# RMSNorm on one core: the fourth tile stored whole, the third loaded in two halves, five rows of the last group on GpSimd

## The chip, the core and the metric

The kernel runs on one NeuronCore of a Trainium2 chip. The metric is device time in microseconds (us); before the change the median of 8 runs is 161.97 us, from 161.75 to 163.17. A core has a matrix engine (TensorE, PE), a vector engine (VectorE, DVE), a scalar engine (ScalarE, ACT), GpSimd (POOL), a sync engine (SyncE, SP) that here only issues transfers, and 16 DMA engines that carry all transfers between the off-chip memory (HBM) and the on-chip memory (SBUF). PSUM is the small memory that TensorE writes to.

## The reference

```python
def reference(x, gamma):          # x: (16, 1024, 512) float32, gamma: (512,) float32
    eps = 1e-5
    rms = np.sqrt(np.mean(x ** 2, axis=-1, keepdims=True) + eps)
    return (x / rms * gamma).astype(np.float32)
```

There are 16,384 rows of 512 numbers. Each is divided by its root mean square and multiplied by gamma, element by element. 33.55 MB are read and as much is written.

## The kernel before

**Tiles.** The rows are cut into 4 tiles of 128 partitions x 32 rows x 512 numbers, 8.39 MB each. A partition's 32 rows lie one after another in HBM, 64 KB in one piece. There are three buffers, `slots`; tiles 0, 1 and 2 (called first, second and third below) have one each, and tile 3 (the fourth) reuses the buffer of tile 0 (`slot_of`, line 86).

**Groups.** Compute goes by groups of rows of one tile, listed in `groups` (lines 75 to 85) as tile, first row, number of rows, the pieces in which squares are taken, and `share`: how many of the last rows of the group GpSimd scales. The first tile has groups of 7, 9 and 16 rows, the others two of 16 each.

**One group.** ScalarE squares a piece of rows into a scratch tile, and VectorE sums each row of it (`square_sums`, lines 92 and 93). ScalarE takes the root, and VectorE the reciprocal (`inverse_rms`, lines 98 and 99). GpSimd then multiplies its share of the rows by the reciprocals, and in a second pass by gamma (lines 105 and 106). ScalarE multiplies the other rows by their reciprocal, one instruction for each row (line 114), and when all of these are done, VectorE multiplies them by gamma in one instruction (line 118), which reads gamma from PSUM. While a group is scaled, squares and sums of the next group are mixed in between by the main loop (lines 162 to 178); in the last group nothing is left to mix in.

**Gamma.** It is loaded in five pieces into one partition (lines 53 to 57), spread over 128 partitions by a matmul with a column of ones (line 66), and copied from PSUM to SBUF for GpSimd (line 161).

**Order.** The schedule is manual: every engine's instructions stand in the order of the program, and semaphore waits are added where data depend. All transfers are issued by SP, in program order, so an issue that waits holds all later ones. The first loads are issued at once; all further stores and loads are issued by `transfers` (lines 125 to 145), called after a group's work is written down. After the first group it issues three single-row stores of the first tile between the loads of the third tile, which comes as one half and two quarters. After the third group it issues the stores of the rest of the first tile, and then the loads of the fourth tile into the same buffer, which wait for these stores to have landed. The second and third tile are each stored whole; the fourth is stored in two halves, each after its own group.

Of the kernel before, what the change touches and what calls it, by code (L numbers as in the profile page):

```python
# [9 lines left out]
def kernel(  # L10
# [15 lines left out]
    N, D = xf.shape  # L26
# [17 lines left out]
    def load(t, slot, r0, r1):  # L44
        dma = nc.sync.dma_start(out=slots[slot][:, r0:r1], in_=xv[t][:, r0:r1])
        before_scale.append((slot, r0, r1, dma))

    def store(t, slot, r0, r1):
        dma = nc.sync.dma_start(out=ov[t][:, r0:r1], in_=slots[slot][:, r0:r1])  # L49
        before_scale.append((slot, r0, r1, dma))  # L50

    gamma_row = const.tile([1, D], fp32)
    pieces = (0, 128, 224, 320, 416, D)

    load(0, 0, 0, 8)
    for c0, c1 in zip(pieces, pieces[1:]):
# [24 lines left out]
        (2, 0, 16, (7, 5, 4), 7),  # L81
        (2, 16, 16, (7, 5, 4), 7),
        (3, 0, 16, (7, 5, 4), 7),
        (3, 16, 16, (7, 5, 4), 3),
    ]
    slot_of = [0, 1, 2, 0]

    def square_sums(ss, t, g, r, m, k):
        home, name, most = ((psum, "sq_psum", 7), (const, "sq_sbuf", 5))[k % 2]
        sq = home.tile([P, most, D], fp32, name=name)  # L90
        rows = slots[slot_of[t]][:, g + r : g + r + m, :]
        nc.scalar.activation(out=sq[:, :m], in_=rows, func=AF.Square)  # L92
        nc.vector.tensor_reduce(  # L93
            out=ss[:, r : r + m, 0], in_=sq[:, :m], axis=mybir.AxisListType.X, op=OP.add
        )

    def inverse_rms(ss, n):
        nc.scalar.activation(out=ss[:, :n, 0], in_=ss[:, :n, 0], func=AF.Sqrt, bias=eps_t, scale=1.0 / D)  # L98
        nc.vector.reciprocal(out=ss[:, :n, 0], in_=ss[:, :n, 0])  # L99
        return ss  # L100

    def scale_by_pool(rstd, t, g, n, share):
        part = slots[slot_of[t]][:, g + n - share : g + n, :]
        by_row = rstd[:, n - share : n].to_broadcast([P, share, D])
        nc.gpsimd.tensor_tensor(out=part, in0=part, in1=by_row, op=OP.mult)  # L105
        last = nc.gpsimd.tensor_tensor(  # L106
            out=part, in0=part, in1=gamma_b.to_broadcast([P, share, D]), op=OP.mult
        )
        before_scale.append((slot_of[t], g + n - share, g + n, last))

    def scale(rstd, t, g, r0, r1):
        x = slots[slot_of[t]]
        for r in range(r0, r1):
            nc.scalar.activation(out=x[:, g + r, :], in_=x[:, g + r, :], func=AF.Copy, scale=rstd[:, r])  # L114

    def times_gamma(t, g, r0, r1):
        part = slots[slot_of[t]][:, g + r0 : g + r1, :]
        scaled = nc.vector.tensor_tensor(  # L118
            out=part, in0=part, in1=gamma_psum.to_broadcast([P, r1 - r0, D]), op=OP.mult
        )  # L120
        for slot, b0, b1, earlier in before_scale:
            if slot == slot_of[t] and b0 < g + r1 and g + r0 < b1:
                tc.declare_no_dep(scaled.ins, earlier.ins, reason="ScalarE waited for it before it scaled these rows")

    def transfers(t, g):
        if (t, g) == (0, 0):
            store(0, 0, 0, 1)
            load(2, 2, 0, 16)
            store(0, 0, 1, 2)
            load(2, 2, 16, 24)  # L130
            store(0, 0, 2, 3)
            load(2, 2, 24, 32)
        elif (t, g) == (0, 16):
            store(0, 0, 3, 16)
            store(0, 0, 16, 32)
            load(3, 0, 0, 16)
            load(3, 0, 16, 32)
        elif (t, g) == (1, 16):
            store(1, 1, 0, 32)
        elif (t, g) == (2, 16):  # L140
            store(2, 2, 0, 32)
        elif (t, g) == (3, 0):
            store(3, 0, 0, 16)
        elif (t, g) == (3, 16):
            store(3, 0, 16, 32)

    def pieces_of(group):
        t, g, n, pieces, share = group
        ss = stats.tile([P, 16, 1], fp32, name="ss")
        r = 0  # L150
        todo = []
        for k, m in enumerate(pieces):
            todo.append((ss, t, g, r, m, k))
            r += m
        return ss, todo
# [6 lines left out]
    for k, group in enumerate(groups):  # L162
        t, g, n, pieces, share = group
        mine = n - share
        half = (mine + 1) // 2
        ahead = groups[k + 1 :][:1]
        ss, todo = pieces_of(ahead[0]) if ahead else (None, [])
        scale_by_pool(rstd, t, g, n, share)
        for piece in todo[:2]:
            square_sums(*piece)  # L170
        scale(rstd, t, g, 0, half)
        for piece in todo[2:]:
            square_sums(*piece)
        scale(rstd, t, g, half, mine)
        times_gamma(t, g, 0, mine)
        transfers(t, g)
        for nxt in ahead:
            rstd = inverse_rms(ss, nxt[2])
# [30 lines left out]
```

## Time and profile before

| | before |
|---|---|
| median of 8 runs | 161.97 us |
| the profiled execution | 162.09 us, with a span of 160.1 us |
| busy share DVE / ACT / POOL | 70% / 68% / 66% |
| HBM read, written | 33.56 MB, 33.55 MB |
| mean rate of DMA over the span | 419 GB/s |
| DMA packets' share of 16 engines' span | 98.2% |
| SP's issues for the fourth tile's stores | 123.3 us and 137.97 us |

The span runs from the first to the last instruction of the profiled execution; the device time is some 2 us longer. Times inside the span count from its start. Busy shares are means over the whole span. The DMA rows tell how much of 16 engines' time had packets in it. A packet is one contiguous piece moved by one DMA engine: here one partition's part of one transfer. Issuing a transfer takes SP about 0.4 us; "to landing" is the time from the issue until the completion arrived.

### The profile page before, as it was taken

What the parts mean: (1) busy time and instruction counts of PE and PEld (TensorE: products, weight loads), DVE (VectorE), ACT (ScalarE), POOL (GpSimd) and SP (SyncE); (2) the same over time, 40 slices, a digit from 0 to 9 for tenths busy, and PEclk for the clock granted to TensorE, in tenths of its full rate; (3) what the DMA queues carried; (4) which work ended last, traced back from release to release, by engine and by line L of the source; (5) the groups of instructions that cost most, each with busy time, mean ns of one, the idle gap of its engine ahead of it and who ended that gap; (6) DMA issues with size and microseconds to landing.
All of it is one profiled execution on the core that took longest, in us unless ns stands there. A gap on an engine that the chain in (4) does not pass through costs nothing.

```text
span 160.1 us, 280 instructions
## 1 busy us (share of the span) xinstructions
PE 2.0 (1%) x2; PEld 0.5 (0%) x2; DVE 112.5 (70%) x42; ACT 108.1 (68%) x111; POOL 106.4 (66%) x24
## 2 busy tenths in 40 slices
PE   0050000000000000000000000000000000000000
PEld 0010000000000000000000000000000000000000
DVE  0018597997989999999999999899996039400000
ACT  3072989859999998998999499999933960000000
POOL 1000956986998699999999999999999930000000
DMA  5999999999999999999999999996996997999994
GB/s 194 426 438 483 426 393 450 467 393 393 459 393 404 448 442 398 452 410 508 409 393 467 450 393 393 524 508 278 524 508 278 524 475 311 393 475 442 393 450 205
DMA packets 2747, 67.12 MB, mean 419 GB/s; under 512 B 313, under 2 KB 314, under 8 KB 698
## 3 DMA queue, kind: packets, MB, share of 16 engines
q1 hardware_dynamic: 2746, 67.11, 98.2%
q14 instruction: 1, 0.01, 0.0%
HBM read 33.56 MB, written 33.55 MB: 419 GB/s over the span
## 4 chain that ended last, share of the span: by engine, by line
DMA 38%; DVE 29%; ACT 16%; issue 2%; ACTq 0%; SPq 0%
DMA out_dram<-slot 21%; DMA slot<-in_x_dram 17%; DVE ss L93 17%; DVE slot L118 12%; ACT slot L114 8%; ACT sq_psum L92 6%; ACT sq_sbuf L92 1%; ACTq L204 0%; ACT ss L98 0%; ACT gamma_b L161 0%; DVE ss L99 0%; SPq L49 0%; ACTq L92 0%
## 5 line engine op out<-in xcount | busy, mean ns | idle before, releaser
L105 POOL TENSOR_TENSOR slot<-slot,ss 128x3584 f32<-128x3584 f32 (+2 forms) x9 | 46.9, 5214 | 21.9 <-DVE ss L99 21.9
L93 DVE TENSOR_REDUCE ss<-sq_psum 128x7 f32<-128x3584 f32 (+1 forms) x16 | 49.1, 3072 | 16.5 <-ACT sq_psum L92 16.4
L106 POOL TENSOR_TENSOR slot<-slot,gamma_b 128x3584 f32<-128x3584 f32 (+2 forms) x9 | 59.2, 6583 | 0.7
L114 ACT ACTIVATE slot<-slot,ss 128x512 f32<-128x512 f32 x75 | 47.4, 706 | 4.7 <-DVE ss L99 4.7
L118 DVE TENSOR_TENSOR slot<-slot,gamma_psum 128x4608 f32<-128x4608 f32 (+2 forms) x9 | 41.3, 4591 | 8.5 <-ACT slot L114 8.5
L92 ACT ACTIVATE sq_psum<-slot 128x3584 f32<-128x3584 f32 (+1 forms) x16 | 40.2, 2511 | 8.4 <-DMA slot<-in_x_dram 7.0
L93 DVE TENSOR_REDUCE ss<-sq_sbuf 128x5 f32<-128x2560 f32 x8 | 22.5, 2807 | 0.0
L92 ACT ACTIVATE sq_sbuf<-slot 128x2560 f32<-128x2560 f32 x8 | 18.6, 2321 | 0.0
L98 ACT ACTIVATE ss<-ss,eps_t 128x16 f32<-128x16 f32 (+2 forms) x9 | 2.7, 303 | 8.4 <-DVE ss L93 8.4
L99 DVE RECIPROCAL ss<-ss 128x16 f32<-128x16 f32 (+2 forms) x9 | 2.1, 236 | 0.4 <-ACT ss L98 0.4
L66 PE MATMUL gamma_psum<-gamma_row,ones_col 1*128 1x512 f32 x2 | 2.0, 1122 | 9.0 <-DMA gamma_row<-in_gamma_dram 9.0
L72 ACT ACT_TABLE_LOAD x1 | 1.3, 1283 | 1.2 <-PEq L193 1.2
L161 ACT COPY gamma_b<-gamma_psum 128x512 f32<-128x512 f32 x1 | 0.6, 567 | 0.0
L66 PEld LDWEIGHTS gamma_psum<-gamma_row,ones_col 1*128 1x128 f32 x2 | 0.5, 305 | 9.0 <-issue 9.0
L64 POOL MEMSET ones_col<- 1x128 f32 x1 | 0.2, 194 | 0.3 <-POOLq L193 0.3
L193 POOL MEMSET const-float32-0.0<- 128x1 f32 x1 | 0.1, 98 | 0.2 <-issue 0.2
L72 ACT ACTIVATE table<-eps_t 128x1 f32<-128x1 f32 x1 | 0.2, 202 | 0.0
L193 POOL MEMSET const-bfloat16-1.0<- 128x1 bf16 x1 | 0.1, 101 | 0.0
L193 POOL MEMSET const-uint8-127<- 128x1 uint8 x1 | 0.1, 101 | 0.0
L193 POOL MEMSET const-float32-1.0<- 128x1 f32 x1 | 0.1, 98 | 0.0
L70 POOL MEMSET eps_t<- 128x1 f32 x1 | 0.1, 89 | 0.0
## 6 DMA issues: line engine op xcount, KB each, us to landing
slot<-in_x_dram SPq DMA_DIRECT2D x6, 4096.0 KB, 21.9
out_dram<-slot SPq DMA_DIRECT2D x3, 4096.0 KB, 23.8
slot<-in_x_dram SPq DMA_DIRECT2D x4, 2048.0 KB, 10.2
out_dram<-slot SPq DMA_DIRECT2D x1, 3328.0 KB, 34.3
out_dram<-slot SPq DMA_DIRECT2D x3, 256.0 KB, 31.7
gamma_row<-in_gamma_dram SPq DMA_DIRECT2D x4, 0.4 KB
out_dram<-slot SPq DMA_DIRECT2D x2
gamma_row<-in_gamma_dram SPq DMA_DIRECT2D x1, 0.5 KB
```

The lines of the kernel that those rows point to most:

```text
L66: nc.tensor.matmul(gamma_psum[:, 0], ones_col, gamma_row, start=True, stop=True)
L72: nc.scalar.activation(out=table, in_=eps_t, func=AF.Sqrt)
L92: nc.scalar.activation(out=sq[:, :m], in_=rows, func=AF.Square)
L93: nc.vector.tensor_reduce(out=ss[:, r : r + m, 0], in_=sq[:, :m], axis=mybir.AxisListType.X, op=OP.add)
L98: nc.scalar.activation(out=ss[:, :n, 0], in_=ss[:, :n, 0], func=AF.Sqrt, bias=eps_t, scale=1.0 / D)
L99: nc.vector.reciprocal(out=ss[:, :n, 0], in_=ss[:, :n, 0])
L105: nc.gpsimd.tensor_tensor(out=part, in0=part, in1=by_row, op=OP.mult)
L106: last = nc.gpsimd.tensor_tensor(out=part, in0=part, in1=gamma_b.to_broadcast([P, share, D]), op=OP.mult)
L114: nc.scalar.activation(out=x[:, g + r, :], in_=x[:, g + r, :], func=AF.Copy, scale=rstd[:, r])
L118: scaled = nc.vector.tensor_tensor(out=part, in0=part, in1=gamma_psum.to_broadcast([P, r1 - r0, D]), op=OP.mult)
L161: nc.scalar.copy(out=gamma_b[:, 0], in_=gamma_psum[:, 0])
L193: nc = _bacc.Bacc("TRN2", target_bir_lowering=False, num_devices=1)
```

## The change

Four things are changed. Gamma is loaded in seven pieces instead of five, one of 128 numbers and six of 64. Of the three single-row stores after the first group two stay, the third row goes with the next store of that tile, and rows 16 to 31 of the third tile are loaded in one transfer instead of two. The store of the first half of the fourth tile is dropped, and the whole tile is stored after the last group. In the last group GpSimd takes five rows instead of three, and VectorE multiplies the other eleven by gamma in two instructions, of six rows and of five, the first placed after ScalarE's first six rows.

```diff
-    pieces = (0, 128, 224, 320, 416, D)
+    pieces = (0, 128, 192, 256, 320, 384, 448, D)
...
-        (3, 16, 16, (7, 5, 4), 3),
+        (3, 16, 16, (7, 5, 4), 5),
...
             store(0, 0, 0, 1)
             load(2, 2, 0, 16)
             store(0, 0, 1, 2)
-            load(2, 2, 16, 24)
-            store(0, 0, 2, 3)
-            load(2, 2, 24, 32)
+            load(2, 2, 16, 32)
         elif (t, g) == (0, 16):
-            store(0, 0, 3, 16)
+            store(0, 0, 2, 16)
             store(0, 0, 16, 32)
             load(3, 0, 0, 16)
             load(3, 0, 16, 32)
...
-        elif (t, g) == (3, 0):
-            store(3, 0, 0, 16)
         elif (t, g) == (3, 16):
-            store(3, 0, 16, 32)
+            store(3, 0, 0, 32)
...
         scale(rstd, t, g, 0, half)
+        if not ahead:
+            times_gamma(t, g, 0, half)
         for piece in todo[2:]:
             square_sums(*piece)
         scale(rstd, t, g, half, mine)
-        times_gamma(t, g, 0, mine)
+        times_gamma(t, g, 0 if ahead else half, mine)
         transfers(t, g)
```

## The prediction

> **What bounds the kernel now.** I read the page's slices of the span first. The rows are engines, each digit the busy tenths of a 4 us slice:
>
> ```profile
> DVE  0018597997989999999999999899996039400000
> ACT  3072989859999998998999499999933960000000
> POOL 1000956986998699999999999999999930000000
> DMA  5999999999999999999999999996996997999994
> GB/s 194 426 438 483 426 393 450 467 393 393 459 393 404 448 442 398 452 410 508 409 393 467 450 393 393 524 508 278 524 508 278 524 475 311 393 475 442 393 450 205
> ```
>
> The compute engines start late and stop five slices before the end. DMA is full from the second slice to the last but one; the few sixes sit beside slices over the mean and are not gaps, as the stretches below explain. Next the page's part on queues:
>
> ```profile
> DMA packets 2747, 67.12 MB, mean 419 GB/s; under 512 B 313, under 2 KB 314, under 8 KB 698
> q1 hardware_dynamic: 2746, 67.11, 98.2%
> ```
>
> 98.2% of 160.1 us is 157.2 us of packet time on each of 16 engines. The trace's single packet records begin at 1.74 us and end at 158.90, which is 157.16 us: no engine is ever without a packet in between.
>
> The chain of waits points elsewhere. Its last pieces (start, length, what) are
>
> ```profile
> 122.73 1.33 ACT slot L114 x2
> ...
> 124.67 6.13 ACT slot L114 x10
> 130.80 0.02 issue
> 130.82 7.09 DVE slot L118
> ```
>
> It is followed back from the last instruction and stops at 137.9; the 22 us behind it are not in it. What they are is shown by the table of stretches (the last two columns are DMA share and GB/s):
>
> ```profile
> 110.00:137.00 27.00, 0.00 (x0) 0.00 (x0) 18.87 (x6) 15.15 (x23) 19.35 (x4) 1.00 1.06 461
> 137.00:138.00 1.00, 0.00 (x0) 0.00 (x0) 0.91 (x1) 0.00 (x0) 0.00 (x0) 1.00 0.15 66
> 138.00:158.00 20.00, 0.00 (x0) 0.00 (x0) 0.00 (x0) 0.00 (x0) 0.00 (x0) 1.00 0.97 419
> 158.00:159.00 1.00, 0.00 (x0) 0.00 (x0) 0.00 (x0) 0.00 (x0) 0.00 (x0) 1.00 0.01 0
> ```
>
> A packet is booked whole to the stretch it starts in, so shares over 1 occur and a thin us is no gap. 20 us at 419 GB/s are 8.38 MB: all of the fourth tile (8.39 MB), the half issued at 123.3 as well as the half issued at 137.97. So the third tile's store kept the engines until about 138.9 (its 64 KB packets take 2.42 us each, and the last start just after 136 to 137), and the half issued at 123.3 had waited 15 us in the queue. The bound is bytes over the DMA engines, not the arithmetic.
>
> **What the Trainium skill says.** "DMA: Bandwidth & Descriptors", section "Where 436 GB/s comes from": 16 ports give 435 GB/s, and for transfers between HBM and SBUF a lower HBM limit of about 358 binds. The trace sides with the first: share 1.00 goes with 428 to 435 GB/s. The same page, "Why small descriptors are slow (HBM only)": a packet has a fixed overhead. The trace agrees: 24.4 GB/s per engine in 2 KB packets, 26.8 in 16 KB, 27.0 in 32 KB, 27.1 in 64 KB. The same page, "Why a DMA increments its semaphore by 16 and not by 1": a DMA runs on k engines set by its outer dimension, each ending with a semaphore write. The count of 313 small packets agrees: 19 large DMAs x 16, plus 5 + 4 for gamma's pieces on one engine.
>
> **The change part by part,** against the profiled span of 160.1 us (first packet at 1.74, last at 158.90, 1.2 us to the end). That execution took 162.09 us, 0.12 above the median of 161.97. Packet lengths are medians of the packet records: 84 ns for 2 KB, 611 for 16 KB, 987 for 26 KB, 1213 for 32 KB, 2418 for 64 KB, 9 for a semaphore write. Each engine carries 8 of a DMA's 128 packets.
>
> *Gamma in 7 pieces instead of 5.* SP issues five in 1.58 us (timeline), so two more cost 0.63 us, and every later issue of the first batch moves: the next load goes out at 3.4 instead of 2.79. It is hidden by the first load, whose packets last until 7.1 to 7.7; without that cover 0.63 us would be lost. On the one engine that carries gamma, a piece with its semaphore takes 25 ns in the records: +0.05 us, and that engine ends last, I infer from its order in the records. Matmul L66, which waits until 9.03, moves by the same; its product is read at 15.40.
>
> *One single-row store fewer.* 8 x 84 = 0.67 us per engine goes. The row rides in the larger store, where 6 KB more cost 226 ns between the 26 KB and 32 KB packets, hence 75 per 2 KB, x8 = 0.60. Gain 0.07 at most, since the 2 KB records overlap a little; 0.03 at least. SP loses one issue of 0.38 us, ahead of the last load of the third tile. The row leaves with rows 3 to 15, issued at 37.34 in either case; the load of tile 4 into these rows waited for that store (it landed 34.3 us later), not for row 2.
>
> *Rows 16 to 31 of the third tile in one load.* 16 x 611 = 9.78 becomes 8 x 1213 = 9.70: -0.07. The squares that need it start at 75.8; the later half landed 36.2 us after 27.4, at 63.6. Cover 12 us.
>
> *The fourth tile stored whole.* 16 x 1213 = 19.41 becomes 8 x 2418 = 19.34: -0.06. The half that could go at 123.3 now waits for the last compute, so that is worked out. Rstd is ready at 122.7. ACT: 11 rows at 8.06/13 = 0.62, six by 126.45, eleven by 129.55. DVE: 6 rows at 7.09/13 = 0.545 plus a start, 126.5 to 129.8, then 5 rows to 132.6. POOL is free at 123.24 and does five rows as in the second group of the first tile, 4.46 + 5.60 (timeline): 133.3. POOL is last; SP issues at about 133.4, 4.6 us before the old last store. From issue to first packet took 1.0 us at the start (0.73 to 1.74), so packets can start at 134.4. The engines are with the third tile until about 138.9: 4.5 us of cover, and a gap of 0. Nothing is gained from the earlier issue either, because the store stands behind the third tile's. Without the cover each us later would be a us of loss.
>
> *Semaphore writes.* Three large DMAs fewer, 9 ns each per engine: -0.03. The final wait is for one DMA instead of two; nothing priced.
>
> Sum: +0.05 - 0.07 - 0.07 - 0.06 - 0.03 = -0.18 us. With records that overlap by some ns the packet savings may be half of that; bounds -0.3 and 0. I take -0.15: span 159.95, and 161.8 us against the median.
>
> **Rivals.**
>
> *The compute end sets the time.* The chain of waits speaks for it; the compute end moves by 4.6 us, giving 157.4. Against it stand the 8.39 MB still to be moved at 138, with no idle engine before. Chance 0.02.
>
> *Large DMAs cost more than their packets show.* The skill's page (section "Anatomy of one DMA") puts some 2 us of fixed cost on each, mostly completion. If 0.2 us of it blocked the engines, three fewer would give -0.6 more: 161.2. Against it: packets of neighbouring DMAs follow each other at once in the records. Chance 0.05.
>
> *The tail runs dry (slower).* The whole store waits for POOL, and the queue empties. It decides once the last issue comes after about 137.9: POOL would need over 14.6 us for its ten row passes against 10.06 seen. Even a seven-row share (6.16 + 7.8 from 123.24) ends at 137.2. POOL at twice its time ends at 143.4, a gap of 5.5 us, 167.3. A stall elsewhere in the last group has the same threshold. Chance 0.04.
>
> *The diff does nothing measurable:* this is my forecast's mechanism with the size at zero, 162.0, and is inside it.
>
> **How the numbers follow.** The forecast case, DMA full throughout and a saving of 0 to 0.3 us, has 0.89. A measurement of this kernel can tell about 0.3%, 0.49 us, from no change. Inside the forecast case the runs of before (161.75 to 163.17, most within 0.2 of 162) leave 0.04 on the faster side and 0.02 on the slower. Faster: 0.02 + 0.05 + 0.04 = 0.11; slower: 0.04 + 0.02 = 0.06; same: 0.83. The range is the forecast's bounds, 161.67 to 161.97, widened by some 0.25 for the median's own scatter: 161.4 to 162.2.
>
> **What would show it.** The stretches from 2 to 158 us should keep shares near 1.00 with none empty between 134 and 140; packets fall by 48 semaphore writes, rise by 4 for gamma, and lose 128 rows and 256 large ones. SP's last issue should stand near 133.4, released by POOL L106, with some 25 us from issue to landing instead of 21.3. The squares of tile 4 should start near 91.1 as before. The prediction is wrong if the last store's packets start later than about 139, if the large packets come out slower than 2.42 us, or if the span shrinks with the compute end.

## The result and the profile after

The changed kernel takes 164.23 us (median of 11 runs, 163.98 to 164.31) against 161.87 before (32 runs, the eight of the table above among them). The ratio is 1.0135, interval 1.0116 to 1.0154: 1.9 to 2.5 us slower, where a change between nothing and 0.3 us faster was forecast. The profiled span grew from 160.1 to 162.2 us.

The page of the changed kernel, busy tenths of DMA in 40 slices and the queue's share:

```profile
DMA  5789899899998999999989989959959969979983
...
q1 hardware_dynamic: 2318, 67.11, 97.1%
```

The bytes are the same, and the packets are as many as worked out (2746 - 48 + 4 - 128 - 256 = 2318), but their share of the span fell from 98.2% to 97.1%: the engines stood empty somewhere. The second and third slices show it, 7 and 8 where before had 9 and 9. (The five and the sixes further on are no gaps: a packet is booked where it starts, as the prediction says of the kernel before.)

SP's issues at the start tell why. Columns are start and length in us, then the engine and line, and how many issues. Before:

```profile
0.73 0.38 SPq L45 DMA_DIRECT2D slot<-in_x_dram  x1
1.16 1.58 SPq L57 DMA_DIRECT2D gamma_row<-in_gamma_dram  x5
2.79 6.09 SPq L45 DMA_DIRECT2D slot<-in_x_dram  x4
```

After:

```profile
0.74 0.38 SPq L45 DMA_DIRECT2D slot<-in_x_dram  x1
1.18 2.10 SPq L57 DMA_DIRECT2D gamma_row<-in_gamma_dram  x7
7.91 1.89 SPq L45 DMA_DIRECT2D slot<-in_x_dram  x4
```

Gamma's pieces took 0.5 us more, where 0.63 was priced. But then SP stood still, and the second load went out at 7.91 instead of about 3.4. What it waited for is in the table of SP's own waits, in the first 20 us of the changed kernel (us in total, how many waits, the longest):

```profile
SPq L45 <- DMA slot<-in_x_dram: 4.6, 1, 4.6
```

A load waited for a load, though the two write different rows. The table of stretches of the changed kernel shows what that did (last two columns: DMA share and GB/s):

```profile
7.00:8.00 1.00, 0.00 (x0) 0.00 (x0) 0.00 (x0) 0.08 (x1) 0.00 (x0) 1.00 0.02 2
8.00:9.00 1.00, 0.06 (x1) 0.09 (x1) 0.00 (x0) 1.00 (x1) 0.00 (x0) 1.00 0.32 82
9.00:10.00 1.00, 1.00 (x2) 0.40 (x2) 0.00 (x0) 1.00 (x1) 0.00 (x0) 1.00 1.00 229
```

The same three in the kernel before:

```profile
7.00:8.00 1.00, 0.00 (x0) 0.00 (x0) 0.00 (x0) 0.00 (x0) 0.00 (x0) 1.00 0.97 412
8.00:9.00 1.00, 0.00 (x0) 0.01 (x1) 0.00 (x0) 0.92 (x1) 0.00 (x0) 1.00 0.99 426
9.00:10.00 1.00, 0.97 (x1) 0.49 (x2) 0.00 (x0) 1.00 (x1) 0.00 (x0) 1.00 1.07 459
```

In the changed kernel, from 7 to 9 us, (1 - 0.02) + (1 - 0.32) = 1.66 us are empty. From 9 to 10 the engines are full again but move 229 GB/s instead of the 433 that go with a full share elsewhere, which loses another 0.47 us. The sum, 2.1 us, is the growth of the span.

The reason for the wait stands in the program as built. A semaphore is a counter that a transfer raises when it has landed, and for which an engine can wait. The program gives the transfers issued by SP eight semaphores in turn, and a transfer that takes a semaphore a second time waits until its earlier user has landed. The first transfers of the changed kernel and what they wait for:

```
L45 load rows 0-7 of the first tile      semaphore 0
L57 gamma, seven pieces                  semaphores 1 to 7
L45 load rows 8-15                       waits for semaphore 0
L45 load rows 16-31                      waits for semaphore 1
```

In the kernel before, with five pieces, the load of rows 8 to 15 takes semaphore 6 and that of rows 16 to 31 semaphore 7; the first that must wait is the load of the second tile. It waited too, as SP's waits of the kernel before show:

```profile
SPq L45 <- DMA slot<-in_x_dram: 4.4, 1, 4.4
```

But the loads of rows 8 to 31, 6.3 MB, were in the queue ahead of its data, so the wait was hidden.

The tail did what was forecast, 2.4 us later. Timeline of the changed kernel:

```profile
125.64 4.45 POOL L105 TENSOR_TENSOR slot<-slot,ss 128x2560 f32<-128x2560 f32 x1
...
130.18 5.62 POOL L106 TENSOR_TENSOR slot<-slot,gamma_b 128x2560 f32<-128x2560 f32 x1
135.82 0.33 SPq L49 DMA_DIRECT2D out_dram<-slot  x1
```

and its stretches:

```profile
110.00:136.00 26.00, 0.00 (x0) 0.00 (x0) 21.36 (x9) 16.52 (x23) 25.17 (x5) 1.00 0.97 421
136.00:160.00 24.00, 0.00 (x0) 0.00 (x0) 0.00 (x0) 0.00 (x0) 0.00 (x0) 1.00 1.01 437
```

GpSimd's two passes over five rows took 4.45 + 5.62 us, and it was the last engine. DMA is full on both sides of the last issue.

### The profile page after: what moved, and what is told of

Its sections match the earlier page's. It is cut to its first block, busy times and chain, and to the rows that moved or that the text cites. A ratio compares the mean times of both kernels' runs of the same rounds, so it can differ in the third digit from the quotient of the medians.

```text
span 162.2 us, 278 instructions
## 1 busy us (share of the span) xinstructions
PE 2.0 (1%) x2; PEld 0.5 (0%) x2; DVE 111.5 (69%) x43; ACT 107.0 (66%) x109; POOL 110.3 (68%) x24
## 3 DMA queue, kind: packets, MB, share of 16 engines
q1 hardware_dynamic: 2318, 67.11, 97.1%
## 4 chain that ended last, share of the span: by engine, by line
DMA 48%; POOL 11%; DVE 10%; ACT 8%; POOLq 3%; issue 2%; SPq 0%; ACTq 0%
DMA slot<-in_x_dram 27%; DMA out_dram<-slot 22%; POOL slot L105 7%; DVE ss L93 5%; POOL slot L106 5%; DVE slot L118 4%; POOLq L202 3%; ACT slot L114 3%; ACT sq_psum L92 3%; ACT sq_sbuf L92 1%; SPq L45 0%; DVE ss L99 0%; SPq L49 0%; POOLq L105 0%; ACTq L92 0%
## 5 line engine op out<-in xcount | busy, mean ns | idle before, releaser
L105 POOL TENSOR_TENSOR slot<-slot,ss 128x3584 f32<-128x3584 f32 (+2 forms) x9 | 48.6, 5403 | 24.2 <-DVE ss L99 24.2
L106 POOL TENSOR_TENSOR slot<-slot,gamma_b 128x3584 f32<-128x3584 f32 (+2 forms) x9 | 61.4, 6825 | 0.7
L114 ACT ACTIVATE slot<-slot,ss 128x512 f32<-128x512 f32 x73 | 46.2, 706 | 4.7 <-DVE ss L99 4.7
L118 DVE TENSOR_TENSOR slot<-slot,gamma_psum 128x4608 f32<-128x4608 f32 (+3 forms) x10 | 40.3, 4039 | 4.2 <-ACT slot L114 4.2
```

What stands on the lines that cost most here:

```text
L106: last = nc.gpsimd.tensor_tensor(out=part, in0=part, in1=gamma_b.to_broadcast([P, share, D]), op=OP.mult)
L118: scaled = nc.vector.tensor_tensor(out=part, in0=part, in1=gamma_psum.to_broadcast([P, r1 - r0, D]), op=OP.mult)
```

## The experiments

Three theories were put on record. A: the reused semaphore makes the second load wait for the first to land. B: the two more pieces cost by themselves. C: the rest of the change costs the time.

**The rest of the change alone.**

```diff
-    pieces = (0, 128, 192, 256, 320, 384, 448, D)
+    pieces = (0, 128, 224, 320, 416, D)
```

> The changed kernel with gamma in five pieces again; all else of the change stays. Theory A (a semaphore that is reused makes the second load wait for the first to land, because the first load and seven pieces use up all eight): the second load goes out near 2.8 us, no empty stretch at 8 to 9 us, 161.7 us, so 0.0 to 0.3 below the kernel before. Theory B (the two more pieces cost by themselves, as issues and small packets): also about 161.7. Theory C (the whole-tile store, the merged load or the tail cost the time): stays near 164.2.

Measured: 161.62 us, 1.0007 of before (0.9998 to 1.0016). Theory C falls. SP's second load went out at 2.91, and the last store at 133.40, the time worked out in the prediction. The saving of some 0.2 us summed for merged transfers is not seen: this interval leaves at most 0.03 us. (That of the run with one piece below, which holds the same rest of the change, leaves up to 0.2.)

**Seven pieces alone,** in the kernel before.

```diff
-    pieces = (0, 128, 224, 320, 416, D)
+    pieces = (0, 128, 192, 256, 320, 384, 448, D)
```

> The kernel before with gamma in seven pieces, nothing else changed. Theory A: the second load is issued near 7.9 us, DMA stands empty for some 1.7 us, 164.1 to 164.4 us. Theory B: the same, 164.1 to 164.4. Theory C: 161.9, as before.

Measured: 164.10 us, 1.0156 (1.0143 to 1.0170). The one edit carries all of the loss. SP's timeline has the second load at 8.01.

**Six pieces,** in the kernel before: `pieces = (0, 128, 192, 256, 320, 384, D)`.

> The kernel before with gamma in six pieces. Theory A: the second load is the eighth transfer and takes the last free semaphore, so it goes out near 3.1 us; the third load waits for the first to land, but the second covers that: 161.9 us, within 0.3 of before. Theory B: half of the loss of two pieces, about 163.0. Theory C: 161.9.

Measured: 161.66 us, 1.0001 (0.9993 to 1.0009). Not half the loss but none of it: a step between six pieces and seven, which a price per piece can't give. SP's issues:

```profile
1.17 1.94 SPq L57 DMA_DIRECT2D gamma_row<-in_gamma_dram  x6
3.16 6.17 SPq L45 DMA_DIRECT2D slot<-in_x_dram  x4
```

**One piece,** in the changed kernel: `pieces = (0, D)`.

> The changed kernel with gamma in a single piece. Theory A: no load waits for a load before the first store; the second load is issued near 1.6 us; 161.6 to 161.8 us, no faster than with five pieces since DMA is full in either case. Theory B: each piece fewer than seven gives 1.1 us, so less than 160. Theory C: near 164.2.

Measured: 161.48 us, 0.9995 (0.9987 to 1.0003). All five loads are issued by 3.4 us with no wait, and nothing is gained by it, since DMA was already full.

**The pieces issued by another engine,** in the changed kernel.

```diff
-        nc.sync.dma_start(out=gamma_row[:, c0:c1], in_=gamma.unsqueeze(0)[:, c0:c1])
+        nc.scalar.dma_start(out=gamma_row[:, c0:c1], in_=gamma.unsqueeze(0)[:, c0:c1])
```

> The changed kernel with its seven gamma pieces issued by ScalarE instead of SP. Theory A, with the eight semaphores shared by both issuing engines: SP's second load still waits for the first to land although nothing stands between them on SP; issue near 7.9 us, about 164.2 us. Theory B, if the cost is SP's issue time: the second load goes out near 1.2 us, about 161.8 us.

Measured: 163.82 us, 1.0127 (1.0108 to 1.0146). SP had nothing but loads to issue, and still its second went out at

```profile
7.68 0.33 SPq L45 DMA_DIRECT2D slot<-in_x_dram  x1
```

SP's issue time isn't the cost. But the wait was not the one that the expectation named. SP's waits in the first 20 us:

```profile
SPq L45 <- DMA gamma_row<-in_gamma_dram: 6.6, 1, 6.6
SPq L45 <- DMA slot<-in_x_dram: 0.3, 1, 0.3
```

In this program as built, ScalarE's first piece has the first of the eight semaphores and the first load the second. So SP's second load waited for a gamma piece that another engine had issued: the eight are shared by what SP and ScalarE issue. By the packet records that piece was moved only at 7.11 us, at the end of the first load's packets, and so the second load came as late as in the changed kernel. The same edit with `nc.gpsimd` instead:

> The changed kernel with its seven gamma pieces issued by GpSimd, whose transfers use other semaphores in the built program. Theory A: the second load goes out near 1.2 us, DMA is never empty, 161.6 to 162.0 us. Theory B, if the cost is that of seven small transfers on the DMA engines: near 164.2 us.

Measured: 161.74 us, 0.9983 (0.9964 to 1.0002). Here too there are seven pieces, but their semaphores are others. They are also cut finer, into 224 packets with their semaphore writes, on a queue of their own:

```profile
0.74 2.49 SPq L45 DMA_DIRECT2D slot<-in_x_dram  x5
1.24 3.54 POOL L57 DMA_DIRECT2D gamma_row<-in_gamma_dram  x7 [0.79 <-POOLq L191]
```

```profile
q0 software_dynamic: 224, 0.00, 0.1%
```

SP's issues run through without a wait. More small packets than in the changed kernel cost nothing here, so the two runs together leave little of theory B.

**The second load ahead of the pieces,** in the changed kernel.

```diff
     load(0, 0, 0, 8)
+    load(0, 0, 8, 16)
     for c0, c1 in zip(pieces, pieces[1:]):
         nc.sync.dma_start(out=gamma_row[:, c0:c1], in_=gamma.unsqueeze(0)[:, c0:c1])
-    load(0, 0, 8, 16)
     load(0, 0, 16, 32)
```

> The changed kernel with the second load issued ahead of the seven gamma pieces. Theory A: the wait for the first load to land falls on the seventh gamma piece; the third load is held to about 8.5 us, but the second load keeps DMA full until about 12 us: 161.6 to 162.0 us. Gamma lands some 4 us later and is still ahead of its first reader at 15. Theory B: near 164.2 us, since all pieces are there.

Measured: 164.03 us, 1.0136 (1.0121 to 1.0151), a miss. I had followed only the first reuse, not the next one. Gamma's seventh piece does wait for the first load, but the third load is the tenth transfer and waits for the second, which by then is this order's second load. SP's issues and the stretches:

```profile
12.96 1.30 SPq L45 DMA_DIRECT2D slot<-in_x_dram  x3
```

```profile
12.00:13.00 1.00, 0.00 (x0) 0.00 (x0) 1.00 (x1) 0.00 (x0) 0.00 (x0) 1.00 0.02 2
13.00:14.00 1.00, 0.00 (x0) 0.00 (x0) 1.00 (x1) 0.00 (x0) 0.00 (x0) 1.00 0.47 131
```

The same hole stands at 12 us instead of 7. So the rule is sharper than the theory put it: each transfer waits for the one eight places before it, and time is lost where that one lands only when the queue has run dry. Seven small transfers between two loads on SP, here as in the changed kernel, make it so.

**The pieces spread,** a test of that rule: all seven on SP, the second load between the fourth and fifth.

```diff
-    for c0, c1 in zip(pieces, pieces[1:]):
+    cuts = list(zip(pieces, pieces[1:]))
+    for c0, c1 in cuts[:4]:
         nc.sync.dma_start(out=gamma_row[:, c0:c1], in_=gamma.unsqueeze(0)[:, c0:c1])
     load(0, 0, 8, 16)
+    for c0, c1 in cuts[4:]:
+        nc.sync.dma_start(out=gamma_row[:, c0:c1], in_=gamma.unsqueeze(0)[:, c0:c1])
```

> The changed kernel with the second load placed between the fourth and the fifth of the seven gamma pieces; all pieces stay on SP. Theory A, as the run with the second load first corrected it (each transfer waits for the one eight before it; time is lost only where a load so waits for the load right ahead of it in the queue): the seventh piece waits for the first load, the third load for a gamma piece, both near 8 us, while the second load fills DMA until 12: no hole, 161.5 to 161.9 us. Theory B (seven pieces on SP cost, wherever they stand): near 164.1.

Measured: 161.64 us, 1.0000 (0.9983 to 1.0018). SP still waits until about 8 us, with its queue covered by the second load:

```profile
2.39 0.36 SPq L45 DMA_DIRECT2D slot<-in_x_dram  x1
2.79 5.57 SPq L61 DMA_DIRECT2D gamma_row<-in_gamma_dram  x3
8.40 1.29 SPq L45 DMA_DIRECT2D slot<-in_x_dram  x3
```

The stretches from 7 to 8 and from 8 to 9 us, empty in the changed kernel, have shares of 0.93 and 1.03 here.

As many pieces, as many issues, as many waits and no loss: theory B is gone, and the wait itself costs nothing while another load is in the queue.

**A longer first load,** in the changed kernel: `load(0, 0, 0, 12)` and `load(0, 0, 12, 16)`.

> The changed kernel with a first load of 12 rows instead of 8 and a second of 4. Theory A: the price is the turnaround from the last packet of one load over its landing and the next issue to the first packet, not the size of the load: the same hole of 1.7 us moves to about 10 to 12 us, 164.0 to 164.5 us. If the price grew with the load that is waited for, it would be 165 us or more; if a longer first load covered the wait, 161.8.

Measured: 164.26 us, 1.0154 (1.0137 to 1.0171). The hole moved, and its price stayed:

```profile
9.00:10.00 1.00, 0.00 (x0) 0.00 (x0) 0.00 (x0) 0.00 (x0) 0.00 (x0) 1.00 0.31 125
10.00:11.00 1.00, 0.00 (x0) 0.00 (x0) 0.00 (x0) 0.55 (x1) 0.00 (x0) 1.00 0.00 0
11.00:12.00 1.00, 0.57 (x1) 0.49 (x2) 0.00 (x0) 1.00 (x1) 0.00 (x0) 1.00 0.76 147
12.00:13.00 1.00, 1.00 (x2) 0.00 (x0) 0.00 (x0) 1.00 (x1) 0.00 (x0) 1.00 0.75 311
```

Here 0.69 + 1.00 + 0.24 + 0.25 us are below a full share, some of it because a packet is booked where it starts. The price is the turnaround, not the length of the load that is waited for: by the packet records, 1.3 us pass from the end of the first load's last packet over its landing and the next issue to the next load's first packet, here (10.10 to 11.43 us) as in the changed kernel (7.57 to 8.89 us).

**The cover in the tail.** The prediction held that the whole-tile store is free because the third tile's store keeps DMA busy until about 138.9. In the changed kernel with five pieces:

```diff
-        (3, 16, 16, (7, 5, 4), 5),
+        (3, 16, 16, (7, 5, 4), 9),
```

> The changed kernel with gamma in five pieces and nine rows instead of five on GpSimd in the last group, so that the whole-tile store is issued late. GpSimd's passes: 9 x 0.88 + 9 x 1.11 = 17.9 us from 123.3, ending at 141.2; first packet 1.0 us later. If the tail is covered by the third tile's store until about 138.7, the hole is 3.5 us: 165.0 to 165.6 us. If the end followed the compute end from five rows (133.3), it would be 7.9 us later, 169.5. If the last store's issue time mattered nowhere, 161.6.

Measured: 164.71 us, 1.0180 (1.0166 to 1.0195), thus 2.7 to 3.2 us over before. SP's last issue and the stretches around it:

```profile
141.08 0.33 SPq L49 DMA_DIRECT2D out_dram<-slot  x1
```

```profile
136.00:137.00 1.00, 0.00 (x0) 0.00 (x0) 0.00 (x0) 0.00 (x0) 1.00 (x1) 1.00 2.42 1049
137.00:138.00 1.00, 0.00 (x0) 0.00 (x0) 0.00 (x0) 0.00 (x0) 1.00 (x1) 1.00 0.00 0
138.00:139.00 1.00, 0.00 (x0) 0.00 (x0) 0.00 (x0) 0.00 (x0) 1.00 (x1) 1.00 0.00 0
139.00:140.00 1.00, 0.00 (x0) 0.00 (x0) 0.00 (x0) 0.00 (x0) 1.00 (x1) 1.00 0.01 0
140.00:141.00 1.00, 0.00 (x0) 0.00 (x0) 0.00 (x0) 0.00 (x0) 1.00 (x1) 1.00 0.00 0
141.00:142.00 1.00, 0.00 (x0) 0.00 (x0) 0.00 (x0) 0.00 (x0) 0.05 (x1) 1.00 1.84 786
```

The line to watch is the one with 2.42: sixteen large packets start between 136 and 137 and last 2.42 us, so the engines are busy until about 139. The next start in 141 to 142. An issue 7.7 us later than with five rows (141.08 against 133.40) costs 3.0 us of span (162.8 against 159.8): the cover is real, about 4.7 us. The time lies 0.3 us below the range that was expected, for three small reasons: GpSimd ended at 141.05 instead of 141.2, the first packet came 0.83 us after the issue by the packet records instead of 1.0, and the third tile's store ended at 139.0 instead of 138.7.

No run was clearly faster than the kernel before: the interval of each run without a hole holds 1.

## Why the prediction was wrong

**The bound was right.** It said that bytes over the DMA engines set the time and that compute has slack. Every run with DMA full came out between 0.998 and 1.001, and every run with a hole was slower by that hole.

**The step that failed is "Gamma in 7 pieces instead of 5".** It priced two issues at 0.63 us, put the next load at 3.4 us and called that hidden by the first load's packets. The two issues took 0.5 us, but the load went out at 7.91. What the step left out is a wait that the change adds: with eight transfers ahead of it, the second load waits for the first to land. Thus the cover that the step named was itself what it waited for. The term should have been +2.1 us (1.66 of empty engines and 0.47 of slow restart).

**Where it could be seen.** The profile of before showed the wait. SP had a load waiting for a load for 4.4 us, which no data explains. The line from which the prediction took its 2.79 has four issues in 6.09 us, where one takes about 0.4. And the program as built lists what each transfer waits for. The prediction went by the order of the instructions and not by their waits. No rival was a wait at the start: the one that ended slower put the dry queue at the tail, with the right mechanism (DMA empty) in the wrong place, so the range had nothing above 162.2.

**The tail was right.** Eleven rows on ScalarE, 4.46 + 5.60 us on GpSimd and an issue near 133.4 were met within 0.1 us once the start was mended, and the cover within 0.2 us of the 4.5 given.

**The small savings were not seen.** The sum of some 0.2 us for merged transfers came from lengths of packet records, and these overlap: in the kernel before, 16 KB packets start 0.607 us apart, with records of 0.611. Without the added pieces each DMA engine carries 27 packets fewer ((2746 - 2314) / 16). At 4 ns each, an estimate from these records, 0.1 of the 0.2 us was overlap and no time. Whether the rest is there stays open, since the run with five pieces leaves 0.03 us of it and the run with one piece 0.2. The bounds given, -0.3 and 0, held only at the upper end, and only without the added pieces.

## What to carry to other kernels

Count transfers, not only bytes: where the built program hands out semaphores in turn, the one that comes round again waits for its earlier user, and seven tiny transfers between two loads can turn a full queue into a serial one. Look in the waits of the issuing engine for a load that waits for a load, ask what covers it, and compare the waits of the built program, not only its order, before a change is called free. Where transfers set the end, a late issue is priced by what is still queued ahead of it: 7.7 us of delay cost 3.0 here, and an issue 4.6 us earlier than before (133.40 against 137.97) gained nothing.

## What the runs showed of the hardware that was not expected

Loads that start on empty DMA engines start slowly: in the first us after the hole, a full share went with 229 GB/s instead of 433, and by the packet records the first ten of 16 KB took 0.83 to 1.29 us instead of 0.61. It is the same at the start of the program, in the kernel before too (records of 0.8 to 1.4 us). The store that started on empty engines in the run with nine rows did not show it (its first 64 KB packets took 2.45 to 2.46 us, against 2.42). Why loads are slow to start, no run here tells.
